# The low parts of the first projection chunk's weights: from GpSimd alone to VectorE and GpSimd in turn

## The chip, the core and the metric

The kernel runs on one core of a Trainium2 chip. Its time is the device time of one execution in microseconds (us), as the median of several runs. The core has TensorE (PE in the profile; PEld is its weight load), VectorE (DVE), ScalarE (ACT), GpSimd (POOL) and SyncE (SP), which here issues all DMAs. Each engine works through its own list of instructions in order; an instruction that waits for another engine holds up all that stand behind it on its list.

## What is computed

One decoder layer with two groups of attention heads side by side, for 1024 tokens of width 1024 in float32. The input is normalised, multiplied by one wide input projection, and the columns of the product go to the heads:

```python
h = rms_norm(x, norm_g[layer])
proj = h @ w_in[layer]
dq, dk, dv, dz, nq, nkv, nz, ng = jnp.split(proj, IN_SPLITS, axis=-1)
...
o_diff = diff_attention(dq, dk, dv, lam, diff_slopes)
...
o_nsa = g[0] * o_cmp + g[1] * o_slc + g[2] * o_win
...
x = x + jnp.concatenate([o_diff, o_nsa], axis=-1) @ w_out[layer]
```

The `nkv` columns (768 of them) are the keys and values of the second group, native sparse attention: a compressed branch, a branch over selected blocks and a sliding window. The first 384 of these columns are the first chunk that the kernel projects.

## The kernel before

**Products in three terms.** TensorE multiplies in a shortened float32 format (fp32r). To keep the accuracy, each operand is split into a high part, which is the value rounded to fp32r, and a low part, which is the value minus the high part. A product is then three matmuls: high times high, weight low times token high, weight high times token low (`mm_tokens`, lines 211 to 213).

**Tokens.** `load_x` (lines 228 to 245) treats one of eight token tiles of 128 tokens: it loads `xt`, takes the sum of squares on ScalarE (`xs`, line 235), the power -0.5 on GpSimd (`xr`, line 238), scales the tile on VectorE (line 239), turns it on TensorE in two halves of four transposes (`Tp`, line 155, two PSUM buffers), and takes the high part `xh` on ScalarE (line 244) and the low part `xl` on VectorE (line 245). The next half can be turned only when `xl` has been taken from the buffer before the last.

**Weights.** `load_w` treats a chunk of up to 512 columns in eight blocks `k` of 128 rows: a DMA into `raw` (four buffers, line 192), the high part `whi` on ScalarE (line 202), the low part `wlo` on GpSimd (line 203). `raw` of block `k` is free again when `wlo` of block `k - 4` has been taken. The first chunk (`w_c0`, 384 columns) is loaded together with token tiles 1 to 3, which is what the argument `between` of `load_w` does; only this call passes it. The second chunk (`w_c1`, 408 columns) is called for at token tile 3 of the first chunk's matmuls.

**Who sets the order.** The kernel is written with a scheduler that simulates the whole program and decides, engine by engine, in which order the instructions stand. An edit in one place can so move instructions in quite another. The lists below are what it made of both versions.

**Later stages that matter here.** After eight projection chunks the attention of the second group runs over eight query tiles `qt` (from line 690). Each has a compressed branch, whose probabilities `pg` are turned (line 696), copied to SBUF as `pcT` on ScalarE (line 698) and multiplied by the compressed values (line 700); then softmaxes, whose exponentials are on ScalarE (line 471). In the first two query tiles the output weights are loaded too: `wrow` by DMA (two buffers), its high part `woh` on ScalarE (line 488), its low part `wol` on VectorE (line 490).

Of the kernel before, what the change touches and what calls it, by code (L numbers as in the profile page):

```python
# [8 lines left out]
F32 = mybir.dt.float32  # L9
F32R = mybir.dt.float32r  # L10
AF = mybir.ActivationFunctionType
ALU = mybir.AluOpType
# [15 lines left out]
def block_kernel(ctx: ExitStack, tc: tile.TileContext, x, norm_g, w_in, dq_g, dk_g, lq1, lk1, lq2, lk2,  # L28
                 sub_g, nq_g, nk_g, cmp_pos, cmp_w1, cmp_b1, cmp_w2, w_out, out):
    nc = tc.nc  # L30
# [136 lines left out]
    with ExitStack() as p1:  # L167
# [16 lines left out]
        def load_w(wk, c0, c1, extra=None, perm=False, between={}):  # L184
            n = c1 - c0
            hi = wk.tile([128, 8, 512], F32R, tag="whi", name="whi")
            lo = wk.tile([128, 8, 512], F32R, tag="wlo", name="wlo")
            for k in range(8):
                for tt in between.get(k, ()):
                    load_x(between["xp"], tt)  # L190
                raw = wr.tile([128, 512], F32, tag="raw", name="raw")
                nc.sync.dma_start(raw[:, :n], w_in[128 * k:128 * k + 128, c0:c1])
                m = n
                if extra is not None:
                    m = n + extra[1] - extra[0]
                    nc.sync.dma_start(raw[:, n:m], w_in[128 * k:128 * k + 128, extra[0]:extra[1]])
                h_, l_, r_ = hi[:, k, :m], lo[:, k, :m], raw[:, :m]
                if perm:
                    h_ = h_.rearrange("p (g k d) -> p k g d", g=4, k=2)
                    l_ = l_.rearrange("p (g k d) -> p k g d", g=4, k=2)  # L200
                    r_ = r_.rearrange("p (k g d) -> p k g d", g=4, k=2)
                nc.scalar.activation(h_, r_, AF.Copy)  # L202
                nc.gpsimd.tensor_tensor(l_, r_, h_.bitcast(F32), op=ALU.subtract)  # L203
            return hi, lo

        def mm_tokens(hi, lo, tt, n):
# [21 lines left out]
        def load_x(xp, tt):  # L228
            xt = xp.tile([128, T], F32, tag="xt", name="xt", bufs=5)
            nc.sync.dma_start(xt, x[128 * tt:128 * tt + 128])  # L230
            if tt == 0:
                nc.sync.dma_start(ng_b, bcast(norm_g, 1024))
            xs = xp.tile([128, T], F32, tag="xs", name="xs", bufs=1)
            ss = small.tile([128, 1], F32, tag="xss", name="xss")
            nc.scalar.activation(xs, xt, AF.Square, accum_out=ss)
            nc.vector.tensor_scalar(ss, ss, 1.0 / T, EPS, op0=ALU.mult, op1=ALU.add)
            r = small.tile([128, 1], F32, tag="xr", name="xr")
            nc.gpsimd.tensor_tensor(r, ss, neghalf[:, :1], op=ALU.pow)
            nc.vector.scalar_tensor_tensor(xt, xt, r, ng_b, op0=ALU.mult, op1=ALU.mult)
            t0 = 128 * tt  # L240
            for hf in range(2):
                X3 = transposed(xt[:, 512 * hf:512 * hf + 512], 4)
                k = slice(4 * hf, 4 * hf + 4)
                nc.scalar.activation(xh[:, k, t0:t0 + 128], X3, AF.Copy)  # L244
                nc.vector.tensor_tensor(xl[:, k, t0:t0 + 128], X3, xh[:, k, t0:t0 + 128].bitcast(F32), op=ALU.subtract)


        with ExitStack() as pc:
            xp = pc.enter_context(tc.tile_pool(name="xp", bufs=1))
            ng_b = xp.tile([128, 1024], F32, name="ng_b")  # L250
            load_x(xp, 0)
            w_c0 = load_w(wB, C_NKV, C_NKV + 384, between={"xp": xp, 3: (1,), 5: (2,), 7: (3,)})
            load_gains(1, nk_g, 3)
            for tt in range(NT):
                if tt + 4 < NT:
                    load_x(xp, tt + 4)
                if tt == 6:
                    load_consts(xp)
                t0 = 128 * tt
                if tt == 3:  # L260
                    w_c1 = load_w(wA, C_NKV + 384, C_NKV + 768, extra=(C_NG, C_NG + 24))
                A = mm_tokens(*w_c0, tt, 384)
                raw = st.tile([128, 512], F32, tag="qn", name="kvraw", bufs=3)
                nc.scalar.activation(raw[:, :256], A[:, :256], AF.Copy)
                kn = rms_heads(st, A[:, 256:384], 2, None)
                kvt = st.tile([128, 4, 128], F32, tag="z", name="kvt")[:, :2]
                nc.vector.tensor_copy(kvt, transposed(raw, 2))
                nc.sync.dma_start(kv_d[:, :, t0:t0 + 128].rearrange("b p t -> p b t"), kvt)
                k_pairs(kn, 1, G_KS, "nk", 0, tt)


        w_nq = load_w(wB, C_NQ, C_NQ + 512)

        cctx = ExitStack()
# [557 lines left out]
```

## Time and profile before

| | |
|---|---|
| Median of 3 runs | 807.11 us (806.10 to 807.27) |
| Profiled execution, its own time | 807.29 us |
| Its span | 805.6 us |
| TensorE busy | 770.8 us, 96% of the span |
| VectorE busy | 516.6 us |
| ScalarE busy | 356.6 us |
| GpSimd busy | 329.1 us |

The span is the time from the first to the last instruction; the execution's own time has 1.7 us around it. TensorE is busy nearly throughout, so the time can change in two ways only: by the idle stretches of TensorE, of which there are some 35 us in all, and by the stretches in which its clock is low. A matmul of 384 columns is issued every 0.17 us at the high clock and every 0.32 us at the low one.

### The profile page before, as it was taken

To read this page: it belongs to the slowest core of one execution; us is meant where nothing else is said; L and a number is where in the kernel's file an instruction comes from. 1 tells how busy PE (TensorE), PEld (TensorE's weight loads), DVE (VectorE), ACT (ScalarE), POOL (GpSimd) and SP (SyncE) were. 2 spreads that over 40 slices of the span, in tenths; PEclk is the share of its full clock that TensorE was granted. 3 is DMA by queue.
4 is the path that set the end of the run, shared out by engine and by line. 5 is a ranking of instruction groups with operands and counts; after the bars stand their busy time and mean duration, and the time that the engine had idled before them with its cause. 6 is when DMAs were issued, how large, how long until landed. Compare 5 with 4: busy or idle time off the path is not lost. (4 is left out here: it accounts for less than half of the span.)

```text
span 805.6 us, 13024 instructions
## 1 busy us (share of the span) xinstructions
PE 770.8 (96%) x4457; PEld 640.9 (80%) x4457; DVE 516.6 (64%) x1239; ACT 356.6 (44%) x803; POOL 329.1 (41%) x393
## 2 busy tenths in 40 slices
PE   5999999999999999999979999999999999999997
PEld 4899988888888888888757778777777668998885
DVE  4643864488634548941487687786866287789843
ACT  6443322241323223101487557565647276766410
POOL 5816272250625526020256443443342227755321
PEclk9999999999999999999999999999999999999999
DMA  8538675472433545177494232341321815556233
GB/s 286 170 58 244 165 228 140 107 195 100 138 102 112 153 100 136 40 184 207 139 216 123 84 106 81 106 91 56 80 65 34 248 34 183 159 141 172 74 130 111
DMA packets 89297, 106.68 MB, mean 132 GB/s; under 512 B 15120, under 2 KB 62352, under 8 KB 89104
## 3 DMA queue, kind: packets, MB, share of 16 engines
q1 hardware_dynamic: 89232, 105.86, 47.4%
q8 instruction: 35, 0.57, 0.3%
q14 instruction: 30, 0.25, 0.1%
HBM read 72.27 MB, written 33.55 MB: 131 GB/s over the span
## 5 line engine op out<-in xcount | busy, mean ns | idle before, releaser
L471 ACT ACTIVATE P<-P,nm 128x128 f32<-128x128 f32 (+7 forms) x136 | 101.4, 748 | 42.6 <-DVE nm L469 39.0
L203 POOL TENSOR_TENSOR wlo<-raw,whi 128x512 fp32r<-128x512 f32 (+2 forms) x64 | 85.7, 1363 | 53.1 <-ACT whi L202 51.3
L522 ACT ACTIVATE pT<-Tp 128x512 f32<-128x512 f32 (+3 forms) x118 | 66.3, 573 | 72.9 <-PE Tp L649 60.4
L138 POOL TENSOR_TENSOR r<-ss,neghalf 128x8 f32<-128x8 f32 (+2 forms) x41 | 51.0, 1244 | 112.6 <-DVE ss L136 107.6
L211 PE MATMUL S<-whi,xh 128*128 128x512 f32 (+2 forms) x224 | 86.5, 386 | 0.6 <-ACT xh L244 0.6
L211 PE MATMUL A<-whi,xh 128*128 128x512 f32 (+2 forms) x224 | 86.8, 388 | 0.0
L213 PE MATMUL A<-whi,xl 128*128 128x512 f32 (+2 forms) x224 | 86.4, 386 | 0.0
L212 PE MATMUL S<-wlo,xh 128*128 128x512 f32 (+2 forms) x224 | 86.3, 385 | 0.0
L213 PE MATMUL S<-whi,xl 128*128 128x512 f32 (+2 forms) x224 | 86.0, 384 | 0.0
L212 PE MATMUL A<-wlo,xh 128*128 128x512 f32 (+2 forms) x224 | 85.6, 383 | 0.0
L618 POOL TENSOR_SCALAR P<-P,ssum 128x128 f32<-128x128 f32 (+7 forms) x72 | 52.2, 743 | 76.4 <-DVE ssum L614 44.2
L469 DVE CUSTOM_DVE_ANT_0 P<-S,D 128x128 f32<-128x128 f32 (+7 forms) x96 | 60.3, 661 | 22.7 <-PE S L465 14.1
L465 PE MATMUL S<-nsaK,QH 128*128 128x384 f32 (+2 forms) x192 | 68.2, 363 | 0.7 <-DVE nm L469 0.7
L654 PE MATMUL A<-pT,vsw 128*64 128x256 f32 x528 | 65.4, 386 | 2.0 <-ACT P L471 1.2
L465 PE MATMUL S<-nsaK,QL 128*128 128x384 f32 (+2 forms) x192 | 60.4, 329 | 0.0
L618 POOL TENSOR_SCALAR Pw<-Pw,ssum 128x640 f32<-128x640 f32 (+3 forms) x56 | 39.8, 730 | 47.7 <-DVE ssum L614 39.8
L163 DVE RECIPROCAL e<-e 128x512 f32<-128x512 f32 (+1 forms) x18 | 57.1, 3175 | 0.5
L520 DVE COPY pT<-Tp 128x512 f32<-128x512 f32 (+3 forms) x62 | 38.5, 620 | 28.3 <-PE Tp L649 28.2
L202 ACT ACTIVATE whi<-raw 128x512 fp32r<-128x512 f32 (+2 forms) x64 | 36.5, 606 | 44.1 <-DMA raw<-in_w_in_dram 38.1
L654 PEld LDWEIGHTS A<-pT,vsw 128*64 128x64 f32 x528 | 34.6, 136 | 25.3 <-ACT pT L522 2.7
L502 PE MATMUL A<-woh,ch 128*128 128x512 f32 x128 | 51.7, 404 | 1.9 <-ACT ch L748 1.5
L504 PE MATMUL A<-woh,cl 128*128 128x512 f32 x128 | 50.3, 395 | 0.1
(189 smaller groups left out, 1772.4 us busy)
## 6 DMA issues: line engine op xcount, KB each, us to landing
raw<-in_w_in_dram SPq DMA_DIRECT2D x48, 256.0 KB, 3.1
xt<-in_x_dram SPq DMA_DIRECT2D x16, 512.0 KB, 3.8
w<-in_cmp_w_dram SPq DMA_DIRECT2D x16, 256.0 KB, 3.8
QH<-nqs_d SPq DMA_DIRECT2D x16, 256.0 KB, 5.3
QL<-nqs_d SPq DMA_DIRECT2D x16, 256.0 KB, 6.6
xa_d<-xt SPq DMA_DIRECT2D x16, 256.0 KB, 2.0
QH<-dqs_d SPq DMA_DIRECT2D x16, 256.0 KB, 5.3
QL<-dqs_d SPq DMA_DIRECT2D x16, 256.0 KB, 7.1
```

Of the source, the lines that this page charges most:

```text
L163: nc.vector.reciprocal(e, e)
L203: nc.gpsimd.tensor_tensor(l_, r_, h_.bitcast(F32), op=ALU.subtract)
L211: nc.tensor.matmul(A[:, :n], a, hi[:, k, :n], start=(k == 0), stop=False)
L212: nc.tensor.matmul(A[:, :n], a, lo[:, k, :n], start=False, stop=False)
L213: nc.tensor.matmul(A[:, :n], b, hi[:, k, :n], start=False, stop=(k == 7))
L465: nc.tensor.matmul(S[a][:, c0:c1], Q[:, heads[a]], Ks[a][:, w0 + c0 - o:w0 + c1 - o], start=Q is QH, stop=Q is QL)
L469: nc.vector.tensor_tensor_reduce(out=Ps[a][:, :n], in0=S[a][:, o:o + n], in1=biases[a], scale=-slopes[a], scalar=3e38, op0=ALU.add, op1=AL ...
L471: nc.scalar.activation(Ps[a][:, :n], Ps[a][:, :n], AF.Exp, scale=-1.0, bias=nm, accum_out=ssums[a])
L502: nc.tensor.matmul(A, ch[:, k], woh[:, k, c], start=(k == 0), stop=False)
L522: nc.scalar.activation(pT[:, :n], Tp[:, :n], AF.Copy)
L618: nc.gpsimd.tensor_scalar(P[:, :n], P[:, :n], ssum[:, g2, j:j + 1], 1.0, op0=ALU.mult, op1=ALU.mult)
L654: nc.tensor.matmul(O[64 * j:64 * j + 64, 256 * gp:256 * gp + 256], vsw[:, br, k0 + kt, 64 * j:64 * j + 64], pT[:, 256 * j:256 * j + 256], ...
```

## The change

In the blocks of the first chunk, and only there, the low parts of the odd blocks (`k` = 1, 3, 5, 7) are taken on VectorE; the even ones stay on GpSimd. The two lines that are added move all later line numbers up by two, so that line 203 (`wlo`) is line 205 after the change, 238 (`xr`) is 240, 698 (`pcT`) is 700.

```diff
@@ -200,7 +200,9 @@
                     l_ = l_.rearrange("p (g k d) -> p k g d", g=4, k=2)
                     r_ = r_.rearrange("p (k g d) -> p k g d", g=4, k=2)
                 nc.scalar.activation(h_, r_, AF.Copy)
-                nc.gpsimd.tensor_tensor(l_, r_, h_.bitcast(F32), op=ALU.subtract)
+
+                eng = nc.vector if between and k % 2 else nc.gpsimd
+                eng.tensor_tensor(l_, r_, h_.bitcast(F32), op=ALU.subtract)
             return hi, lo
```

What the scheduler makes of it is shown at three places. The first is GpSimd's list in the first 35 us: `wlo` of width 384 belongs to the first chunk, of width 408 to the second, `xr` to the token tiles 0 to 7 in turn, `r` to the first projected tile. Before:

```order
L238 TENSOR_TENSOR xr<-xss,neghalf 128x1
L203 TENSOR_TENSOR wlo<-raw,whi 128x384 x3
L238 TENSOR_TENSOR xr<-xss,neghalf 128x1
L203 TENSOR_TENSOR wlo<-raw,whi 128x384
L238 TENSOR_TENSOR xr<-xss,neghalf 128x1 x2
L203 TENSOR_TENSOR wlo<-raw,whi 128x384 x2
L238 TENSOR_TENSOR xr<-xss,neghalf 128x1 x2
L203 TENSOR_TENSOR wlo<-raw,whi 128x384 x2
L238 TENSOR_TENSOR xr<-xss,neghalf 128x1
L203 TENSOR_TENSOR wlo<-raw,whi 128x408 x2
L238 TENSOR_TENSOR xr<-xss,neghalf 128x1
L203 TENSOR_TENSOR wlo<-raw,whi 128x408 x3
```

And after:

```order
L240 TENSOR_TENSOR xr<-xss,neghalf 128x1
L205 TENSOR_TENSOR wlo<-raw,whi 128x384 x2
L240 TENSOR_TENSOR xr<-xss,neghalf 128x1 x3
L205 TENSOR_TENSOR wlo<-raw,whi 128x384 x2
L240 TENSOR_TENSOR xr<-xss,neghalf 128x1 x2
L205 TENSOR_TENSOR wlo<-raw,whi 128x408 x2
L240 TENSOR_TENSOR xr<-xss,neghalf 128x1
L205 TENSOR_TENSOR wlo<-raw,whi 128x408 x2
L240 TENSOR_TENSOR xr<-xss,neghalf 128x1
L138 TENSOR_TENSOR r<-ss,neghalf 128x2
L205 TENSOR_TENSOR wlo<-raw,whi 128x408 x4
```

Four `wlo` have gone; the `xr` of token tile 6 now stands behind two low parts of the second chunk instead of none, and that of tile 7 behind four instead of two.

The second place is ScalarE's list at the end of the same stretch: `whi` of width 408 are the high parts of the second chunk, `xh` the high parts of the token halves. Before:

```order
L202 ACTIVATE whi<-raw 128x384 x2
L235 ACTIVATE xs,xss<-xt 128x1024
L244 ACTIVATE xh<-Tp 128x4x128 x2
L202 ACTIVATE whi<-raw 128x408 x2
L118 ACTIVATE lsum<-lsum 128x2
L235 ACTIVATE xs,xss<-xt 128x1024
L202 ACTIVATE whi<-raw 128x408 x2
```

And after:

```order
L202 ACTIVATE whi<-raw 128x384
L237 ACTIVATE xs,xss<-xt 128x1024
L246 ACTIVATE xh<-Tp 128x4x128
L202 ACTIVATE whi<-raw 128x408 x3
L246 ACTIVATE xh<-Tp 128x4x128
L118 ACTIVATE lsum<-lsum 128x2
L237 ACTIVATE xs,xss<-xt 128x1024
```

One of the two `xh` (the first half of token tile 3) now stands behind three high parts of the second chunk.

The third place is ScalarE's list in the second query tile (`qt` = 1) of the sparse attention, some 400 us into the program. Before:

```order
L522 ACTIVATE pT<-Tp 128x512
L471 ACTIVATE Pw,ssum<-Pw,nm 128x256 x2
L471 ACTIVATE P,ssum<-P,nm 128x256 x3
L488 ACTIVATE woh<-wrow 128x512 x2
L698 ACTIVATE pcT<-A 128x512
L471 ACTIVATE P,ssum<-P,nm 128x256 x3
L714 ACTIVATE ch<-nzt 128x512
```

And after:

```order
L524 ACTIVATE pT<-Tp 128x512
L473 ACTIVATE Pw,ssum<-Pw,nm 128x256 x2
L473 ACTIVATE P,ssum<-P,nm 128x256 x3
L490 ACTIVATE woh<-wrow 128x512 x2
L473 ACTIVATE P,ssum<-P,nm 128x256 x3
L700 ACTIVATE pcT<-A 128x512
L716 ACTIVATE ch<-nzt 128x512
```

`pcT` now stands behind three exponentials that stood behind it. TensorE's list is the same at this place, down to the matmul of line 700 that reads `pcT`. Between 35 us and 110 us a few rows are exchanged; from there to about 400 us the lists of all engines are alike; between 430 us and 590 us some rows are exchanged again on all of them.

## Rows read from the trace of the kernel before

**Rows 1.** The page's first part: busy us, share of the span, instructions.
```profile
PE 770.8 (96%) x4457; PEld 640.9 (80%) x4457; DVE 516.6 (64%) x1239; ACT 356.6 (44%) x803; POOL 329.1 (41%) x393
```
**Rows 2.** Waits of TensorE: us in total, times, longest.
```profile
PE Tp L155 <- DVE xt L239: 8.2, 1, 8.2
PE A L700 <- ACT pcT L698: 2.6, 1, 2.6
...
PE Tp L155 <- DVE xl L245: 2.2, 2, 1.2
```
**Rows 3.** Timeline, TensorE near 33 us: start, us, instruction, [idle before <-releaser].
```profile
32.25 0.44 PE L211 MATMUL S<-whi,xh 128*128 128x384 f32 x1 [0.40 <-ACT xh L244]
...
34.08 0.66 PE L155 MATMUL Tp<-ident,xt 128*128 128x128 f32 x4 [1.21 <-DVE xl L245]
```
**Rows 4.** Stretches: length, busy per engine (instructions), granted clock, DMA share, GB/s.
```profile
31.50:34.10 2.60, 1.00 (x6) 0.36 (x4) 2.57 (x5) 1.81 (x5) 2.60 (x2) 1.00 0.44 113
34.97:38.28 3.31, 3.31 (x13) 3.21 (x13) 1.42 (x4) 1.20 (x3) 3.15 (x4) 0.50 0.69 192
...
412.40:415.30 2.90, 0.28 (x3) 0.01 (x1) 1.03 (x2) 1.69 (x4) 0.92 (x3) 1.00 1.04 240
415.30:420.00 4.70, 4.70 (x28) 3.34 (x30) 4.70 (x30) 4.70 (x15) 1.29 (x1) 1.00 0.90 215
```
**Rows 5.** Timeline of VectorE, first 35 us.
```profile
6.86 1.28 DVE L239 SCALAR_TENSOR_TENSOR xt<-xt,xr,ng_b 128x1024 f32<-128x1024 f32 x1 [0.82 <-POOL xr L238]
9.98 0.69 DVE L245 TENSOR_TENSOR xl<-Tp,xh 128x512 fp32r<-128x512 f32 x1 [1.84 <-ACT xh L244]
...
11.84 2.03 DVE L239 SCALAR_TENSOR_TENSOR xt<-xt,xr,ng_b 128x1024 f32<-128x1024 f32 x1 [0.67 <-POOL xr L238]
...
33.34 1.27 DVE L245 TENSOR_TENSOR xl<-Tp,xh 128x512 fp32r<-128x512 f32 x2
```
**Rows 6.** Timeline of GpSimd, 21 to 37 us.
```profile
21.11 3.67 POOL L203 TENSOR_TENSOR wlo<-raw,whi 128x384 fp32r<-128x384 f32 x2
...
29.82 0.55 POOL L238 TENSOR_TENSOR xr<-xss,neghalf 128x1 f32<-128x1 f32 x1
...
35.04 2.06 POOL L203 TENSOR_TENSOR wlo<-raw,whi 128x408 fp32r<-128x408 f32 x2
```
**Rows 7.** Lines 203 and 490 over the span: ns min/median/max, first and last start.
```profile
L203 POOL TENSOR_TENSOR wlo<-raw,whi x64: 998/1294/2805, 7.9 to 314.2; 128x512 fp32r<-128x512 f32 x48, 128x384 fp32r<-128x384 f32 x8, 128x408 fp32r<-128x408 f32 x8
...
L490 DVE TENSOR_TENSOR wol<-wrow,woh x8: 679/686/1479, 403.0 to 419.9; 128x512 fp32r<-128x512 f32 x8
```
**Rows 8.** Timeline of ScalarE, 26 to 31 us.
```profile
26.16 1.09 ACT L202 ACTIVATE whi<-raw 128x408 fp32r<-128x408 f32 x2 [2.91 <-DMA raw<-in_w_in_dram]
...
27.88 1.06 ACT L235 ACTIVATE xs<-xt 128x1024 f32<-128x1024 f32 x1 [0.54 <-POOL wlo L203]
...
30.02 0.55 ACT L202 ACTIVATE whi<-raw 128x408 fp32r<-128x408 f32 x1 [0.55 <-DMA raw<-in_w_in_dram]
30.47 0.37 ACT L264 ACTIVATE kvraw<-A 128x256 f32<-128x256 f32 x1
...
30.89 0.39 ACT L264 ACTIVATE kvraw<-S 128x256 f32<-128x256 f32 x1
```
**Rows 9.** Timeline of SyncE, the issue of the last token tile.
```profile
21.89 0.37 SPq L230 DMA_DIRECT2D xt<-in_x_dram  x1
```
**Rows 10.** DMA issues near 22 us: KB each, us to landing.
```profile
xt<-in_x_dram SPq DMA_DIRECT2D x1, 512.0 KB, 5.9
```
**Rows 11.** Timeline of ScalarE in the second query tile.
```profile
413.61 1.15 ACT L488 ACTIVATE woh<-wrow 128x512 fp32r<-128x512 f32 x2 [3.77 <-DMA wrow<-in_w_out_dram]
414.66 0.58 ACT L698 ACTIVATE pcT<-A 128x512 f32<-128x512 f32 x1
415.14 0.50 ACT L471 ACTIVATE P<-P,nm 128x256 f32<-128x256 f32 x1
...
416.13 0.49 ACT L471 ACTIVATE P<-P,nm 128x256 f32<-128x256 f32 x1
```

## The prediction

> **What bounds the kernel now.** I read the page's first part, then TensorE's waits, then the timeline of each engine around the two waits that the new lists touch. The page: TensorE is busy 770.8 of 805.6 us [rows 1], so only its 35 us of idle time and its time at the low clock can be won, and any longer wait of TensorE is lost in full. Its list of waits is short at the start: 8.2 us until the first token tile is scaled, 2.2 us in two waits for `xl`, and later 2.6 us in a single wait for `pcT`, the longest behind the first [rows 2]. The subtraction on GpSimd, which the change halves, is in no row there: TensorE never waits for `wlo` directly. GpSimd counts only through what stands behind its subtractions. That is seen near 33 us: TensorE waits 0.40 us for an `xh` and then 1.21 us for an `xl`, until 34.08 [rows 3]. It is busy 1.00 of 2.60 us there, and afterwards the granted clock is 0.50, the lower of the two levels (1.2 for 2.4 GHz), for 3.31 us [rows 4]. This place costs 0.40 + 1.21 + 3.31 / 2 = 3.3 us, and it is all that the change could win behind the start.
>
> The `xl` that ends it is the first half of a pair that takes VectorE 1.27 us from 33.34 [rows 5]. It stands on VectorE behind the scaling of token tile 7, which needs `xr` of that tile, which GpSimd gives at 29.82 + 0.55, after two low parts of the second chunk [rows 6].
>
> **What is removed.** Four of 64 subtractions leave GpSimd. One takes 1.0 to 2.8 us there, 1.29 at the median [rows 7], so about 5.2 us of GpSimd's time in the first 25 us; the last two of the eight alone took 3.67 [rows 6].
>
> **What is added.** Four subtractions of 384 columns on VectorE, which the trace does not show there at this width. The same operation with 512 columns takes VectorE 0.68 to 1.48 us, median 0.69 [rows 7]; scaled by 384 / 512 the low end is 0.51 (an estimate), the high end is 1.48. I take 0.55 each, the median scaled and rounded up: 2.2 us in sum, between 2.0 and 5.9. What hides them: `k` = 1 falls into the 1.84 us in which VectorE waits for `xh`, and `k` = 3 into the 0.67 us before the scaling at 11.84 [rows 5]. `k` = 5 and 7 stand between later `xl` and scalings; they push these back, but the scaling beside GpSimd took 2.03 us where one alone took 1.28 [rows 5], and with GpSimd relieved the 0.75 is mostly given back. TensorE's first wait for `xl` (2.2 - 1.21 = 1.0) may so become half a microsecond shorter. That only lets TensorE reach the wait near 33 us sooner: the end of that wait is set by others. I count these edits at nothing; without the cover they would cost up to 4 x 1.48 - 2.2 = 3.7 us of VectorE, of which TensorE would see what passes 34.08.
>
> **What is moved at the start.** The end of the wait near 33 us has to be built anew, since `xr` of tile 7 stands behind four low parts of the second chunk now, and ScalarE has one `xh` behind three of its casts. The last token tile lands at 21.89 + 5.9 = 27.8 us [rows 9, 10]. Its load moves one weight block back on SP's list, and one small load that stood ahead moves behind, so I leave that. ScalarE can cast the second chunk from 26.16, when its first block lands [rows 8]: three casts to 27.7 (1.09 for two, 0.55 for one), the delayed `xh` to about 28.2. Then the squares of tile 7, 1.06 [rows 8]: 29.3. Two evacuations, 30.89 - 30.47 = 0.42 [rows 8]: 29.7. The fourth cast, 0.55: 30.3. Its low part on GpSimd, half of 2.06 [rows 6]: 31.3. `xr`, 0.55: 31.8. The scaling, 1.28 alone: 33.1. `xl`, half of 1.27: 33.75. TensorE goes on a tenth later, at 33.85, against 34.08. If the scaling runs beside a subtraction, as the 2.03 does [rows 5], it is 34.6. I take 34.1, between the two: no change, between -0.2 and +0.5. The work that TensorE has done by then is the same (the transposes of tile 4's second half come as the same item of its list), and the low clock afterwards stays. The outer bounds: -3.3 if the whole place dissolves, and +1.8 if one of the subtractions ahead of `xr` takes 2.8 instead of 1.0.
>
> On the last point the Trainium skill has a rule, page "SBUF — State Buffer", section "Who interferes with whom": a VectorE instruction with two SBUF inputs and a GpSimd instruction that reads SBUF need the same port pair, and whichever starts first holds it to its end. The row of 2.03 us beside 1.28 agrees that such pairs hurt each other. By the rule the scaling of tile 7, which starts ahead of GpSimd's next subtraction, would not be lengthened, and the sum would be 0.2 us lower than mine; by the slow row it would be 0.5 higher.
>
> **What is moved at 413 us.** ScalarE idles 3.77 us until the third block of output weights has landed, casts it from 413.61 on, and then copies `pcT` at 414.66 [rows 11]. TensorE waits 2.62 us for that copy, the 2.6 of rows 2. Now three exponentials stand between the casts and the copy. Two of them take 416.13 - 415.14 = 0.99 us, start to start [rows 11], so three take 1.49. The casts do not move, being tied to a transfer, so `pcT` comes 1.49 us later and TensorE waits 4.1. Nothing covers it: TensorE's next item is the matmul on `pcT`, and behind it TensorE is busy without a gap to 420 us [rows 4]. The exponentials that come earlier by one copy (0.58) serve nobody who waits. Below, this term is 0, if the transfer were early enough; above, the lower clock comes on top (a rival).
>
> **The other exchanged rows** (35 to 110 us, 430 to 590 us) I count at nothing, with 1.2 us either way: the size of one wait such as that of 1.21.
>
> **The sum.** From the profiled execution's 807.29 us: 0 at the start, +1.49 at `pcT`, 0 for the rest: 808.8. The median of the runs is 0.18 lower than that execution, so for a median 808.6.
>
> **The rivals.**
>
> *The start is won.* If loads of the second chunk land 2 us sooner because `raw` is freed sooner, the chain above ends near 32 us, TensorE does not stop and its clock stays up: 807.1 - 3.3 + 1.5 = 805.3. For it: GpSimd loses 5.2 us of work there. Against: ScalarE waits 2.91 us for the landing of the first block [rows 8], and that load was not held by GpSimd's last subtractions.
>
> *The wait at `pcT` does not grow*, because a whole copy of the exponentials' time is lost elsewhere on ScalarE or the weights land early; then nothing is left: 807.1. Against it: the 3.77 us of idle time before the casts.
>
> *The clock falls at `pcT`.* After 1.60 us of idle time in 2.60 the clock fell to 0.50 for 3.31 us; after 2.62 idle in 2.90 it stayed at 1.00 [rows 4]. So it is not the wait's length alone, and with 4.1 us it may go either way. If it falls, it costs a further 3.31 / 2 = 1.65: 810.3. It decides as soon as the rows after that wait show a clock of 0.50.
>
> That the change does not do what it says is out: the four subtractions stand on VectorE's list.
>
> **How the numbers follow.** The forecast has 0.45 (807.8 to 809.4), the start won 0.15, no growth at `pcT` 0.17, the fallen clock 0.23. A measurement of this kernel can tell about 0.2%, 1.6 us: faster is below 805.5, slower above 808.7. The forecast lies at that edge and gives 0.22 to slower and 0.23 to the same; the fallen clock gives 0.22 to slower; no growth gives 0.15 to the same and 0.02 to faster; the start won gives 0.12 to faster and 0.03 to the same; the last hundredth of the fallen clock goes to the same. Together 0.14 faster, 0.42 the same, 0.44 slower. The range runs from 805.4 to 810.6; it leaves out half of the first rival and the end of the third.
>
> **What would show it.** In the changed kernel's profile TensorE's wait for `pcT` should be about 4.1 us, and ScalarE should show three exponentials between the casts and the copy. TensorE should still wait for an `xl` until about 34 us, with a clock of 0.50 behind it. GpSimd's eight low parts of the second chunk should end no sooner than 36 us. VectorE's new subtractions should take 0.5 to 0.6 us each. The prediction is wrong if the wait near 33 us is gone, if the wait at `pcT` is still 2.6 us, or if a wait of over 1 us shows between 430 and 590 us that was not there.

## The result, and the profile after

The changed kernel takes 817.32 us (median of 4 runs, 815.34 to 818.78) against 806.61 us for the kernel before; the ratio is 1.0129, with a 95% interval of 1.011 to 1.0148. The profiled execution took 818.17 us, with a span of 816.4 us: 10.8 us more than the span before. The forecast of 808.6 and its range up to 810.6 were far too low.

The page's first line after the change [rows 1]: busy us, share of the span and instructions.

```profile
PE 774.7 (95%) x4457; PEld 643.3 (79%) x4457; DVE 514.7 (63%) x1243; ACT 357.6 (44%) x803; POOL 324.6 (40%) x389
```

TensorE has the same 4457 matmuls. It is busy 3.9 us longer (more of them at the low clock) and idle 6.9 us longer. The waits of TensorE after, the answer to [rows 2], say where the idle time is:

```profile
PE Tp L155 <- DVE xt L241: 8.3, 2, 8.1
PE S L467 <- DVE nm L471: 5.7, 4, 3.8
PE Tp L155 <- ACT whi L202: 4.9, 1, 4.9
PE S L467 <- DMA QH<-dqs_d: 3.1, 1, 3.1
PE Tp L155 <- DVE xl L247: 2.9, 4, 1.3
...
```

The row with no counterpart before is the third: one wait of 4.9 us, put down to a weight cast (`whi`). (The longest waits for `nm` and `QH` come later, at 424 and 695 us.) It is neither at the start nor at `pcT`; the timeline of TensorE shows it at 67 us, where the first token tile of the second chunk has just ended:

```profile
66.49 0.34 PE L215 MATMUL A<-whi,xl 128*128 128x408 f32 x1
71.77 0.45 PE L155 MATMUL Tp<-ident,qn 128*128 128x128 f32 x1 [4.93 <-ACT whi L202]
72.01 0.63 PE L155 MATMUL Tp<-ident,kvraw 128*128 128x128 f32 x2
```

The stretches from 35 us on, first of before and then of after (columns as in [rows 4]), show the whole early loss: fewer instructions in the first stretch (164 for 177), and in the second 4.93 us idle and a mean clock of 0.77.

```profile
35.00:65.00 30.00, 30.00 (x177) 29.50 (x176) 13.14 (x38) 11.14 (x28) 11.66 (x14) 0.95 0.47 109
65.00:80.00 15.00, 15.00 (x86) 14.58 (x85) 5.67 (x23) 5.82 (x22) 7.77 (x8) 1.00 0.82 251
```

```profile
35.00:65.00 30.00, 28.83 (x164) 26.77 (x163) 11.72 (x33) 10.52 (x27) 7.92 (x9) 0.94 0.40 93
65.00:80.00 15.00, 10.07 (x47) 9.57 (x46) 5.13 (x15) 4.60 (x14) 9.67 (x10) 0.77 0.70 221
```

The account, from the same matmul in both profiled executions. The second chunk's first matmul starts at 58.97 us before and 61.83 after: +2.9. Its third token tile starts at 68.51 and 78.91: +10.4, that is 7.5 more. By the first matmul behind the wait for the compression weights (112.67 and 121.50) the delay is 8.8, in part because that wait is 0.48 us long instead of 1.18. It is 8.7 at 398 us, 11.5 behind the `pcT` of `qt` = 1 (418.52 and 430.05), 9.4 from 571 us on, and 10.9 behind a wait for queries at 690 us.

**The 7.5 us.** ScalarE's timeline after:

```profile
64.89 0.38 ACT L266 ACTIVATE kvraw<-A 128x256 f32<-128x256 f32 x1
69.44 0.63 ACT L202 ACTIVATE whi<-raw 128x512 fp32r<-128x512 f32 x1 [4.17 <-DMA raw<-in_w_in_dram]
69.97 0.26 ACT L133 ACTIVATE qn<-A 128x128 f32<-128x128 f32 x1
```

and before, where the same items stand in another order:

```profile
62.13 0.38 ACT L264 ACTIVATE kvraw<-A 128x256 f32<-128x256 f32 x1
62.40 0.28 ACT L133 ACTIVATE qn<-A 128x128 f32<-128x128 f32 x1
67.08 0.63 ACT L202 ACTIVATE whi<-raw 128x512 fp32r<-128x512 f32 x1 [4.40 <-DMA raw<-in_w_in_dram]
```

Both versions wait more than 4 us for the fifth weight block of the third chunk. Before, the small square `qn` of token tile 6 is taken first and nobody minds the wait; after, it stands behind the waiting cast. From there the wait goes to VectorE, whose next items are these:

```profile
70.26 0.29 DVE L135 TENSOR_REDUCE ss<-qn 128x2 f32<-128x128 f32 x1 [3.51 <-ACT qn L133]
70.58 0.85 DVE L136 TENSOR_SCALAR ss<-ss 128x2 f32<-128x2 f32 x1
71.35 0.28 DVE L146 TENSOR_TENSOR qn<-S,r 128x128 f32<-128x128 f32 x1
```

The last of the three (token tile 5) is what TensorE turns at 71.77. It has nothing to do with the cast: its power `r` was ready at 68.3 us, and from then on it was held up only by its place in VectorE's list. The releaser that the profile names for the 4.93 us, `whi`, is thus two queues away from what TensorE needed.

**The 2.9 us.** TensorE's timeline at a token tile of the first chunk, before:

```profile
48.31 0.60 PE L155 MATMUL Tp<-ident,xt 128*128 128x128 f32 x4
48.67 0.42 PE L211 MATMUL A<-whi,xh 128*128 128x384 f32 x1
```

and after:

```profile
49.09 1.03 PE L155 MATMUL Tp<-ident,xt 128*128 128x128 f32 x8
50.37 0.44 PE L213 MATMUL A<-whi,xh 128*128 128x384 f32 x1 [0.25 <-ACT xh L246]
```

Before, the first four transposes of a tile stand ten matmuls earlier, so that their casts are done in time. After, all eight stand directly ahead of the matmuls that need them. From one `kvraw` copy to the next it takes 5.43 us before (46.58 to 52.01) and 6.26 after (47.80 to 54.06): 2.5 us for three tiles.

### The profile page after: what moved, and what is told of

Read it like the earlier page. It is cut to its first block, busy times and chain, and to the rows that moved or that the text cites. A ratio compares the mean times of both kernels' runs of the same rounds, so it can differ in the third digit from the quotient of the medians.

```text
span 816.4 us, 13029 instructions
## 1 busy us (share of the span) xinstructions
PE 774.7 (95%) x4457; PEld 643.3 (79%) x4457; DVE 514.7 (63%) x1243; ACT 357.6 (44%) x803; POOL 324.6 (40%) x389
## 5 line engine op out<-in xcount | busy, mean ns | idle before, releaser
L205 POOL TENSOR_TENSOR wlo<-raw,whi 128x512 fp32r<-128x512 f32 (+2 forms) x60 | 79.5, 1350 | 63.2 <-ACT whi L202 63.2
L138 POOL TENSOR_TENSOR r<-ss,neghalf 128x8 f32<-128x8 f32 (+2 forms) x41 | 51.0, 1245 | 118.4 <-DVE ss L136 113.8
```

What stands on the lines that cost most here:

```text
L205: eng.tensor_tensor(l_, r_, h_.bitcast(F32), op=ALU.subtract)
```

## The experiments

Theory A: the loss comes from the order that the scheduler gave to all lists after 35 us, not from the moved work. Theory B: it comes from the four subtractions on VectorE. Theory C: the wait at 67 us is a late transfer that comes whatever the order. Theory D: only the transposes count. Each ratio is to the runs of the kernel before on the same chip, with its 95% interval.

**The change, with the transposes kept apart.** One rule for TensorE:

```diff
-                nc.tensor.matmul(A[:, :n], b, hi[:, k, :n], start=False, stop=(k == 7))
+                with tc.issue_after(behind.ins) if behind is not None and k == 4 else ExitStack():
+                    nc.tensor.matmul(A[:, :n], b, hi[:, k, :n], start=False, stop=(k == 7))
...
-                A = mm_tokens(*w_c0, tt, 384)
+                A = mm_tokens(*w_c0, tt, 384, first_half[tt + 1] if 4 <= tt < 7 else None)
```

> The change, and one rule for TensorE alone: in the first chunk's matmuls of token tiles 4 to 6, those from the third of block k = 4 on stand behind the first four transposes of the next token tile. With it the lists of all engines from token tile 4 on, the attention included, are those of the kernel before; only the start, with the four subtractions on VectorE, is that of the changed kernel. Theory A (the loss sits in the order of the lists, not in the moved work): the first chunk's matmuls end near 59.3 us instead of 61.8, the wait of 4.93 us before the third chunk is gone, and the median is 807.0, between 806.0 and 808.5. Theory B (the four subtractions on VectorE and what they do to the start make the loss): at most the 2.5 us of the transposes come back, 814.8 or more. Theory C (the wait of 4.93 us is a late transfer of the third chunk's weights, whatever the order): 814.5.

Measured: 807.61 us, ratio 1.0006 (0.9989 to 1.0022). The whole loss is gone with the four subtractions still on VectorE. Its stretches, like those above:

```profile
35.00:65.00 30.00, 30.00 (x187) 29.58 (x186) 13.70 (x39) 11.14 (x28) 12.22 (x13) 1.00 0.49 114
65.00:80.00 15.00, 14.49 (x82) 13.63 (x81) 5.41 (x23) 5.75 (x22) 7.12 (x7) 1.00 0.77 233
```

B and C fall. ScalarE still waits for the fifth block (5.08 us in this run), with nothing of TensorE's behind it.

**One block only.**

```diff
-                eng = nc.vector if between and k % 2 else nc.gpsimd
+                eng = nc.vector if between and k == 7 else nc.gpsimd
```

> Only one subtraction, that of block k = 7, goes to VectorE. From 35 to 110 us the lists are those of the changed kernel, in the attention those of the kernel before. Theory A: nearly the whole loss of the changed kernel is there, less the 0.7 and 1.4 us that it loses in the attention: 815.2, between 814 and 816.5. Theory B: a quarter of the loss of 10.7: 809.3.

Measured: 815.96 us, ratio 1.0124 (1.0099 to 1.0148), and the same wait of TensorE, 4.68 us at 69.95. One subtraction, which took VectorE 1.38 us here, costs as much as four: the size of the moved work does not matter.

**The change, with the casts as before.**

```diff
+                with tc.issue_after(casts[k].ins) if k in casts else ExitStack():
+                    nc.scalar.activation(h_, r_, AF.Copy)
...
-        w_nq = load_w(wB, C_NQ, C_NQ + 512)
+        w_nq = load_w(wB, C_NQ, C_NQ + 512, casts={k: squares[5 if k < 4 else 6] for k in range(8)}, lows={0: powers[5]})
```

> The change, with the casts and low parts of the third chunk on ScalarE and GpSimd in the order of the kernel before (behind the squares of token tiles 5 and 6, and behind the power of tile 5). The eight transposes of each token tile stay together as in the changed kernel; the attention falls back to the lists of before. Theory A: the 4.93 us and the low clock behind them go (about 7), the 2.5 to 2.9 us of the transposes stay: 809.6, between 808.8 and 811. Theory C: the same wait comes back at the next item that needs those weights: 814 or more.

Measured: 811.57 us, ratio 1.0058 (1.0041 to 1.0075). The wait is gone (15.00 us of 65 to 80 us, 14.95 busy at clock 1.00) and does not come back, so C falls again; the second chunk starts at 61.54, which is the loss of the transposes. The median is 2 us over the expectation and just outside its range. The profiled execution has 0.7 us of that at the compression weights (a wait of 1.89 us there, 1.18 before) and 1.3 us at `pcT`, where the wait was shorter than before (2.29 us) but the clock low behind it. Between 60 and 95 us the lists of TensorE and VectorE are neither those of before nor those of after, so the next experiment is the cleaner one.

**The change, with one exchange on ScalarE.** As above for the fifth block on; no other list moves.

```diff
-        w_nq = load_w(wB, C_NQ, C_NQ + 512)
+        w_nq = load_w(wB, C_NQ, C_NQ + 512, casts={k: squares[6] for k in range(4, 8)}, lows={})
```

> The change, with one exchange on ScalarE's list and none on any other: the square of token tile 6 ahead of the fifth cast of the third chunk's weights instead of behind it. Theory A: VectorE gets the square at 65.2 us instead of 69.97, so that its next item, the scaling of tile 5, only waits for GpSimd's power, which ends at 68.33 behind four low parts; TensorE goes on near 68.65 instead of 71.77: 3.1 us less, 814.2, and 812 if the clock then stays up. Theory C: nothing changes, 817.3.

Measured: 812.46 us, ratio 1.0078 (1.0051 to 1.0104). TensorE's wait, in this run's timeline:

```profile
68.28 0.30 PE L156 MATMUL Tp<-ident,qn 128*128 128x128 f32 x1 [1.96 <-DVE qn L147]
```

The expectation was 1.8 us of waiting until 68.65. The chain from the cast over the square to VectorE's list is shown by this: one position of one 0.26 us instruction takes the ratio from 1.0129 to 1.0078, about 4 us. The wait that is left has another exchange behind it, on GpSimd, where the power `r` of token tile 5 stands behind four low parts (at 67.12 us here; before it stood ahead of them, at 58.67). GpSimd's timeline in this run, and VectorE's:

```profile
62.14 5.02 POOL L208 TENSOR_TENSOR wlo<-raw,whi 128x512 fp32r<-128x512 f32 x4 [3.06 <-ACT whi L204]
67.12 0.70 POOL L139 TENSOR_TENSOR r<-ss,neghalf 128x2 f32<-128x2 f32 x1
```

```profile
67.85 0.29 DVE L147 TENSOR_TENSOR qn<-S,r 128x128 f32<-128x128 f32 x1 [0.66 <-POOL r L139]
```

**The kernel before, with the transposes held together.** No low part leaves GpSimd:

```diff
                 A = mm_tokens(*w_c0, tt, 384)
+                if 4 <= tt < 7:
+                    for t in first_half[tt + 1]:
+                        tc.add_manual_dep(t.ins, last[0].ins.name, ...)
```

> The kernel before, with all low parts on GpSimd, and one rule for TensorE: the first four transposes of token tiles 5, 6 and 7 stand behind the last matmul of the token tile before, so that the eight transposes of a tile stand together as in the changed kernel. No work moves to another engine, and the lists of the start up to token tile 4 are those of before; from there on the scheduler puts all engines into the order of the changed kernel, the attention included. Theory A (order): the whole loss appears without the change, 816.5, between 815 and 818, with a wait of TensorE of 4 to 5 us before the third chunk. Theory B (the moved subtractions): no change, 806.6. Theory D (the order counts, but only the transposes, 0.8 us for each of three tiles): 809.2.

Measured: 816.55 us, ratio 1.0101 (1.0078 to 1.0123). The loss appears without the change:

```profile
71.61 0.45 PE L159 MATMUL Tp<-ident,qn 128*128 128x128 f32 x1 [4.91 <-DVE qn L147]
```

Here the profile puts the wait down to VectorE's `qn`, which TensorE really needs; in the changed kernel it named `whi` for the same wait. Theory A holds in both directions, and D falls: the transposes cost 2.5 us by themselves, and the rule, which touches nothing behind 60 us, changes the third chunk's lists with them.

**The copy `pcT` first** (kernel before):

```diff
             pT = pT_tile("pcT")
-            nc.scalar.activation(pT, Tp, AF.Copy)
+            copy = nc.scalar.activation(pT, Tp, AF.Copy)
+            if qt == 1:
+                for cast in casts[4:]:
+                    tc.add_manual_dep(cast.ins, copy.ins.name, ...)
```

> The kernel before, with the casts of the third and fourth block of output weights behind the copy pcT of query tile 1 on ScalarE. It measures what the wait for pcT is worth, which the prediction let grow. If that wait is set by the casts ahead of it, the copy runs near 410.3 us instead of 414.66, TensorE's 2.62 us go down to under 0.8 and the clock does not fall behind it: 804.5 against 806.4 for before, down to 803 where the clock fell in before's other executions too. If the time comes back because the casts are late for the output projection: 806.4.

Measured: 804.7 us, ratio 0.9958 (0.9936 to 0.998). ScalarE and, behind it, TensorE:

```profile
410.47 0.58 ACT L700 ACTIVATE pcT<-A 128x512 f32<-128x512 f32 x1
414.62 1.15 ACT L490 ACTIVATE woh<-wrow 128x512 fp32r<-128x512 f32 x2 [3.57 <-DMA wrow<-in_w_out_dram]
```

```profile
412.48 1.02 PE L705 MATMUL A<-pcT,vcbd 128*128 128x512 f32 x2
416.50 0.44 PE L466 MATMUL S<-nsaK,QH 128*128 128x384 f32 x1 [1.41 <-DVE nm L470]
```

The time is the expected one, and the copy runs when it was expected to. TensorE does not wait for it any more, but 1.41 us for VectorE a little later, so the wait got smaller rather than going, and stayed over the 0.8 us expected. Against the trace of before, in which the clock had stayed up behind the wait, this execution wins only 0.5 us between 398 and 440 us; the rest of the gain is not seen at this place. The same kind of fault as at 67 us, a small item behind a cast that waits for its weights, was in the kernel before.

**Constants loaded late** (with the copy first). The constants' loads stand behind the second chunk's:

```diff
                 if tt == 6:
-                    load_consts(xp)
+                    with tc.issue_after(raws[-1].ins):
+                        load_consts(xp)
```

> The kernel of the run before in this list (copy pcT first), and the small loads of constants (gains, lambda vectors) behind the last load of the second chunk on SyncE's list. If they hold up the last token tile, which lands at 27.8 us, it lands some 2 us sooner, the stop near 33 us gets shorter than 1 us and the clock behind it stays up: 1.0 to 2.6 us less than without, 802.5. If the second chunk's own loads set it: the same as without, 804.5.

Measured: 809.62 us, ratio 1.0022 (1.0003 to 1.0041): a miss, worse than without. The stop at 34 us stays, and a new one comes, since VectorE's product of the lambda vectors, unmoved on its list, now waits for the late load (2.62 us, until 43.06):

```profile
34.44 0.66 PE L158 MATMUL Tp<-ident,xt 128*128 128x128 f32 x4 [2.07 <-DVE xl L248]
44.33 0.44 PE L158 MATMUL Tp<-ident,kvraw 128*128 128x128 f32 x2 [1.69 <-DVE xl L248]
```

**The same with the change and the transposes apart**, three of the edits above in one kernel:

```diff
+                eng = nc.vector if between and k % 2 else nc.gpsimd
...
+                with tc.issue_after(behind.ins) if behind is not None and k == 4 else ExitStack():
...
+                    with tc.issue_after(raws[-1].ins):
```

> As the run before in this list, but with the four subtractions on VectorE and the rule that keeps the transposes apart: the lists from token tile 4 on are the same in both. It tells what the split itself is worth once no list is upset and the last token tile is early. If GpSimd's relief is of use then, 1 to 2 us less than the run before, 801; if TensorE never waits for GpSimd at the start, the same within 0.8, 802.5; if VectorE's extra 2.2 us push back its low parts of the tokens, 1 us more, 803.5.

Measured: 806.18 us, ratio 0.9981 (0.9963 to 0.9999). That is 3.4 us less than the run before it, but over all three numbers expected: here the stop near 33 us shrinks to 0.83 us, and the new one takes 2.12 us at 41.76, with a low clock behind.

**The change, transposes apart, copy first.** The same without the late constants:

```diff
-                    with tc.issue_after(raws[-1].ins):
-                        load_consts(xp)
+                    load_consts(xp)
```

> The change with both rules that helped: transposes apart, and the copy pcT ahead of the casts. The lists from token tile 4 on are those of the kernel before with the copy first. If the effects add and the split itself is worth nothing: 0.997 of the time before, some 804.2. If the split costs something that the transposes' rule only hid: 806 or more. If it pays: 802.5 or less.

Measured: 805.77 us, ratio 0.9979 (0.996 to 0.9999). It lies between the first two cases expected and shows no gain of the split over the copy alone (0.9958).

**Constants loaded and used late.** `load_consts` is called one tile later, and the product too stands behind the last `xl`. First with all low parts on GpSimd:

```diff
-                if tt == 6:
-                    load_consts(xp)
+                if tt == 7:
+                    with tc.issue_after(raws[-1].ins), tc.issue_after(lows_x[-1].ins):
+                        load_consts(xp)
```

> All low parts on GpSimd, copy pcT first, constants loaded behind the second chunk, and now VectorE's product of the lambda vectors also behind the last xl, so that VectorE does not stop for that late load (that stop took TensorE 1.7 us at 42 to 44 us before). The wait for an xl that ends near 34.4 us was still there with late constants, so it should stay: 804.7, as with the copy first alone. If the late load was all that kept the gain from showing: 802.5.

Measured: 808.97 us, ratio 1.002 (1.0001 to 1.0039), over both expectations: the stop at 34.7 us stayed (1.96 us), and TensorE waited 2.24 us for compression weights at 113.8, with a low clock behind.

Then with the change and the transposes apart as well:

```diff
+                eng = nc.vector if between and k % 2 else nc.gpsimd
...
+                with tc.issue_after(behind.ins) if behind is not None and k == 4 else ExitStack():
```

> The same with the four subtractions on VectorE and the transposes apart. There the wait near 33 us had shrunk to 0.83 us with late constants, and 2.12 us with a low clock behind were lost at 41.8 us instead, to VectorE waiting for the lambda vectors. Without that stop: 2.1 to 3.7 us less than the 806.2 of that run, 802.5 to 804.1. If the stage behind (third chunk, 75 to 85 us) runs at the pace of its own loads, as the lead of 0.9 us that vanished there in the run with the transposes apart says: 804.5, no better than the copy first alone.

Measured: 803.44 us, ratio 0.9953 (0.9934 to 0.9971), level with the copy alone. Against the run before, whose lists are the same from 45 us on, it is 5.5 us less. The spans of the two profiled executions differ by 6.6 us. Of these, 3.3 are there when the second chunk starts (56.32 us, 59.60 without the split), about half of them because the clock stays up behind the stop near 33 us; 3.9 are there at 398 us; the other 2.7 come behind 600 us, where both have the same lists. So the split has a value where the constants come late; how much of the 5.5 us, and that it comes from GpSimd's relief, is not shown. What is won at the start is not kept whole:

```profile
32.97 0.66 PE L161 MATMUL Tp<-ident,xt 128*128 128x128 f32 x4 [1.50 <-DVE xl L256]
109.91 1.67 PE L371 MATMUL S<-flat,w 128*128 128x128 f32 x8 [2.33 <-DMA w<-in_cmp_w_dram]
```

**More buffers for the compression weights.**

```diff
-                w1 = cp.tile([128, 2, 256], F32, tag="w1", name="w1", bufs=4)
+                w1 = cp.tile([128, 2, 256], F32, tag="w1", name="w1", bufs=6)
```

> The run before in this list (the change, transposes apart, copy first, constants loaded and used late), and six buffers instead of four for the weights of the compression (the tile w). That run led the kernel before by 2.6 us at 100 us and had 0.4 us less than nothing of it left at 390 us: TensorE waited 2.33 us at 109.9 us for a load of these weights, and its clock fell behind that. The lists between 100 and 150 us change with it, on TensorE too. If the loads held that lead back: 801.0, about 0.992 of the time before, with no wait over 1 us there. If a new order spends it elsewhere, as the change itself did: 803.4 or more.

Measured: 805.76 us, ratio 0.9992 (0.9973 to 1.001): a miss. In the profiled execution the lead was larger (second chunk at 54.99), and the wait longer, 3.17 us. SyncE's and GpSimd's timelines show what these loads stand behind:

```profile
100.34 3.12 SPq L198 DMA_DIRECT2D raw<-in_w_in_dram  x2
103.88 0.39 SPq L367 DMA_DIRECT2D w<-in_cmp_w_dram  x1
```

```profile
99.05 6.50 POOL L211 TENSOR_TENSOR wlo<-raw,whi 128x512 fp32r<-128x512 f32 x4
```

They stand on SyncE's list behind weight loads whose buffers GpSimd frees, at 1.6 us for a low part. The first item of the attention (`pg` of `qt` = 0) starts at 386.44 us before, 386.17 with the transposes apart, 386.24 here: no profiled execution got there sooner, whatever lead it had at 60 us. That GpSimd's low parts hold the loads is read from this trace; taking some of that later chunk's from GpSimd was not tried.

## Why the prediction was wrong

The start was right. The last wait there ended at 34.49 us instead of 34.08, +0.4 in a range of -0.2 to +0.5, and the clock fell behind it as before. (That it fell was this execution's: in the first experiment, whose lists are the same up to 40 us, it stayed at 1.00 behind a wait of 1.33 us that ended at 34.74.) `xr` of tile 7 ended at 32.5 (31.8 built up), mostly because the last token tile landed at 24.2 + 4.6 = 28.8 us instead of 27.8, its move on SyncE's list having been left out of the sum; the `xl` that TensorE waited for ended at 34.4 (33.75), and GpSimd's low parts of the second chunk at 37.8 (not before 36). A subtraction took VectorE 0.56 to 1.08 us, 0.64 at the median, where 0.55 was taken.

The rule weighed there, that of the Trainium skill ("SBUF — State Buffer", "Who interferes with whom"), can be read in VectorE's rows [rows 5] after:

```profile
28.51 2.08 DVE L241 SCALAR_TENSOR_TENSOR xt<-xt,xr,ng_b 128x1024 f32<-128x1024 f32 x1 [0.26 <-POOL xr L240]
32.55 1.28 DVE L241 SCALAR_TENSOR_TENSOR xt<-xt,xr,ng_b 128x1024 f32<-128x1024 f32 x1 [1.49 <-POOL xr L240]
```

and GpSimd's [rows 6]:

```profile
28.45 1.07 POOL L205 TENSOR_TENSOR wlo<-raw,whi 128x408 fp32r<-128x408 f32 x1
...
32.48 0.70 POOL L138 TENSOR_TENSOR r<-ss,neghalf 128x2 f32<-128x2 f32 x1
33.15 4.64 POOL L205 TENSOR_TENSOR wlo<-raw,whi 128x408 fp32r<-128x408 f32 x4
```

The scaling that started 0.06 us behind a subtraction took 2.08 us, the one that started 0.60 us ahead of one took 1.28. By the rule the later one waits for the pair of ports; for the subtractions the trace agrees, and the prediction's choice of "between the two" was not needed. The small power `r`, which also reads SBUF and started 0.07 us ahead of the second scaling, did not lengthen it.

The step at `pcT` was right on ScalarE; on TensorE only its number was nearly right. The answer to [rows 11]:

```profile
422.39 1.15 ACT L490 ACTIVATE woh<-wrow 128x512 fp32r<-128x512 f32 x2 [3.84 <-DMA wrow<-in_w_out_dram]
424.92 0.57 ACT L700 ACTIVATE pcT<-A 128x512 f32<-128x512 f32 x1
```

From the casts to the copy it is 2.53 us, 1.05 before: +1.48, forecast 1.49. TensorE waited 3.79 us (forecast 4.1), though not for `pcT`. VectorE's list, which the prediction did not weigh here, had changed too: two subtractions that give `nm` stood ahead of the low part `wol`, which waits for the same late casts, and now stand behind it. VectorE before:

```profile
411.24 0.41 DVE L469 CUSTOM_DVE_ANT_0 P<-S,D 128x256 f32<-128x256 f32 x1
...
414.27 0.69 DVE L490 TENSOR_TENSOR wol<-wrow,woh 128x512 fp32r<-128x512 f32 x1 [2.62 <-ACT woh L488]
```

and after, with TensorE behind it:

```profile
423.05 0.69 DVE L492 TENSOR_TENSOR wol<-wrow,woh 128x512 fp32r<-128x512 f32 x1 [3.31 <-ACT woh L490]
423.66 0.42 DVE L471 CUSTOM_DVE_ANT_0 P<-S,D 128x256 f32<-128x256 f32 x1
...
424.49 0.69 PE L467 MATMUL S<-nsaK,QH 128*128 128x384 f32 x1 [3.79 <-DVE nm L471]
```

So the number came about by another path than the forecast's, which is luck. The rival's low clock came as well: 0.51 in the two us behind the wait. Together the delay grew by 2.8 us, from 8.7 to 11.5. Of that 2.1 us came back by 571 us. The same 2.1 us came back in the fourth and fifth experiments, which have the changed kernel's lists in the attention but for a few rows, and nothing in the first three, which have those of before: the exchanged rows of 430 to 590 us won 2.1 us. With the lists of before in this stage the clock fell as well: 0.56, 0.75 and 0.68 behind waits of 2.19, 2.19 and 2.29 us in the first three experiments. The full clock behind 2.62 us in the trace of before was, as far as four traces can tell, one execution's luck.

**The step that failed is "The other exchanged rows (35 to 110 us, 430 to 590 us) I count at nothing, with 1.2 us either way".** From 35 us to the compression weights they cost 8.4 us; from 430 to 590 us they gave back 2.1. The bound was wrong because it was taken from waits of TensorE before. What an exchange can cost is set by the wait that an item is put *behind*, on its own engine: ScalarE's 4.40 us ahead of the fifth cast stood in the trace of before at 67 us, and the list of after had the square behind that cast. The prediction used this reading at 413 us (3.77 us of idle time ahead of the casts) and did not look for it at 67. The rest is the low clock behind so long a stop (2.2 us) and the transposes, moved by ten matmuls, which stood in the comparison of TensorE's lists.

The rival "the start is won" would have failed for another reason, which only the last runs show: most of what is won before 60 us is lost again at 110. The last 1.4 us, at 690 us, stay open. From 600 us on all kernels here have the same lists; yet between 670 and 800 us the changed kernel and the fourth and fifth experiments lose 1.0 to 1.4 us against the trace of before, and the ten others win between 0.1 and 2.9.

## What to carry to other kernels

Where a scheduler orders the lists, an edit's price is not that of the moved instruction: moving a single subtraction of 1.4 us cost 10 us here. Go through each engine's old and new list for items that pass an instruction which *waits* in the trace of before, above all one that waits for a transfer, and price the exchange by that wait and all that stands behind, through every list on the way. Then fix the order with a rule that names two instructions, before judging the work itself.

## What the runs showed of the hardware

The clock behind a stop of the same length, in the same lists, is not the same in each execution. After waits for `pcT` of 2.62, 2.19, 2.19 and 2.29 us it stood at 1.00, 0.56, 0.75 and 0.68 in the two us that followed; after waits for `xl` of 1.32 and 1.33 us near 34 us, in the changed kernel and the first experiment, at 0.73 and 1.00. A stretch such as the 3.31 us at 0.50 of [rows 4] costs half its length, 1.7 us. A difference of that size between two profiled executions is therefore not yet a difference between kernels.
